# Turning the new convolution state on VectorE instead of TensorE, with its stores spread over steps

## The chip, the cores and the metric

The kernel runs on one core of a Trainium2 chip. The core has a matrix engine (TensorE, "PE" in the profile, with its weight loads shown apart as "PEld"), VectorE ("DVE"), ScalarE ("ACT"), GpSimd ("POOL") and SyncE ("SP"), which here only requests DMA transfers. Each engine works through its own queue of instructions in order; an instruction that needs a result of another engine or of a DMA waits at the head of its queue, and all that stands behind it waits too. The metric is the device time of one execution in microseconds (us).

## What is computed

One layer of a streaming encoder is applied to 256 new frames of one stream (the prompt) and to 16 new frames of each of 8 running streams (the sample), 384 rows of 2048 features in all. What matters here is the convolution branch:

```
u   = glu_in[..., :D_CONV] * jax.nn.sigmoid(glu_in[..., D_CONV:])
ext = jnp.concatenate([conv_buf, u], axis=1)            # 30 old rows, then the new ones
z   = layernorm(causal_dwconv(ext, conv_dw_w, conv_dw_b), ...)   # 31 taps, each channel by itself
new_conv = ext[:, -(CONV_W - 1):]                       # the last 30 rows are an output
```

D_CONV is 1024. For the prompt the last 30 rows of `ext` are its last 30 frames. For a sample stream they are 14 old rows and the 16 new ones. Around this stand an input projection, attention, two gates, an output projection and a feed-forward part; all matrix products are made in float32 accuracy, each as three products of a high and a low part.

## The kernel before, in words

The input projection is done panel by panel. Weights come as tiles of 256 rows by 512 columns: SP requests the load into one of three `raw` buffers (line 157), ACT rounds it to the high part `hi` (line 176), DVE subtracts to get the low part `lo` (line 177), and TensorE multiplies `hi` and `lo` (lines 313 to 315, or 318 to 320). There are three buffers for each of `hi` and `lo` (in the GLU stage below a fourth pair in every fourth turn). One call of `gemm` runs over its jobs; after each row block of 128 weights it calls `tick`, which takes one step of the side works. Such a step is called a step here.

Two stages concern us. In the **GLU stage** the 1024 channels of `u` are made with channels on the partitions: four jobs of 16 steps, 12 products of 384 columns in each step, two chunks of 128 channels out of each job. `glu_evac` (lines 783 to 793) takes them out of PSUM on DVE, applies the sigmoid on ACT, and multiplies on POOL into `ut[:, c, :]`, chunk c of eight: 128 channels by 384 rows, the 256 prompt frames first, then 8 streams of 16. Side works of this stage are the attention (`attention`, line 759, a head begins every sixth step) and the convolution (`conv`, line 799). In the **gate stage** after it the two gates are made in eight jobs of 16 steps, nine products of 512 columns in each step; the convolution goes on as a side work and the layer norm over it follows (`conv_branch`, line 932).

The convolution takes chunk c of eight in its turn, 17 steps after the chunk before. `load_state` (line 802) brings the old rows into `sc` by four DMAs 16 steps ahead. `fill` (line 810) builds `ext`, one of two buffers: it transposes `sc` in 32x32 blocks on DVE (line 812) and copies `ut` with shifts on ACT and POOL (lines 814 to 818). It then makes the new state, as channels must become columns: TensorE multiplies two pieces of `ut[:, c]` with the identity into a PSUM tile of the kind `misc` (lines 821 and 822), ACT copies both to `su` (lines 823 and 824), and SP requests two stores to the outputs (lines 825 and 826). Three steps later come the 31 taps, one a step: `tap` (line 828) multiplies a shifted view of `ext` by a column and adds it to `ut[:, c]` on DVE (line 833 for the first tap, 835 for the others). The first tap writes `ut[:, c]`, which is also what lines 821 and 822 read.

TensorE's order is the order of the program text (`tc.manual_schedule(engines={ENG.PE})`, line 381). On the other engines a scheduler orders the instructions when the kernel is built: it simulates the engines, and each engine takes, of what is ready then, the instruction that stands first in the program, where `tc.high_priority` lets the splits, the attention and the evacuations stand some hundred instructions further ahead. On the chip the order is fixed. So DVE's taps need not run in their step: they may come earlier than TensorE's step of the same number, if what they read is there.

The feed-forward part, from about 800 us on, has an order of its own made by a planner; the change does not touch it.

Of the kernel before, what the change touches and what calls it, by code (L numbers as in the profile page):

```python
# [8 lines left out]
F32 = mybir.dt.float32  # L9
# [6 lines left out]
P = 128  # L16
# [25 lines left out]
def hybrid_step(  # L42
# [9 lines left out]
    nc = tc.nc  # L52

    def pool(name, side="left", bufs=1, space=None):
        kw = dict(name=name, bufs=bufs, reuse_waits="tile")
        if space is not None:
            kw["space"] = space
        else:
            kw["side"] = side
        cm = tc.tile_pool(**kw)  # L60
        p = cm.__enter__()
        return p, lambda: cm.__exit__(None, None, None)
# [15 lines left out]
    def misc_tile():  # L78
        made[1] += 1
        return misc.tile([P, 512], F32, tag="misc", name="misc")  # L80
# [13 lines left out]
    tr = nc.tensor.transpose  # L94
# [11 lines left out]
    def queued(d, chain=True):  # L106
        e = d.ins.engine
        if chain and e in newest:
            tc.add_manual_dep(d.ins, newest[e], mybir.DependencyInfo(
                mybir.DependencyClass.NoSync, mybir.DependencyReason.DATA), reason="queue")  # L110
        newest[e] = d.ins.name
# [9 lines left out]
    ident = cp.tile([P, P], F32, name="ident")  # L121
# [306 lines left out]
    p_cv, close_cv = pool("conv", side="right")  # L428
# [116 lines left out]
    def tiny(name):  # L545
        return p_qkv.tile([P, NTT, H], F32, name=name)

    z, e, r, s2, pl = tiny("lz"), tiny("le"), tiny("lr"), tiny("ls"), tiny("lpoly")
# [230 lines left out]
    ut = p_cv.tile([P, 8, NT], F32, name="ut")  # L779
# [17 lines left out]
    nc.gpsimd.memset(sc[:], 0.0)  # L797

    def conv():
        exts = {}  # L800

        def load_state(c):
            for a in range(4):
                o = c * P + 32 * a
                d = nc.sync.dma_start(sc[32 * a:32 * a + 30], state_conv[0, :, :, o:o + 32]
                                      .rearrange("b r d -> r b d"))
                if c == 0:
                    queued(d)

        def fill(c):  # L810
            ext = exts[c] = p_cv.tile([P, 24, 46], F32, tag="ext", bufs=2, name="ext")
            nc.vector.transpose(ext[:, 16:24, 0:32], sc[:])
            u3 = ut[:, c, :].rearrange("p (a t) -> p a t", t=16)
            nc.scalar.copy(ext[:, :, 30:46], u3)
            nc.gpsimd.memset(ext[:, 0, 0:30], 0.0)
            nc.gpsimd.memset(ext[:, 1, 0:14], 0.0)
            nc.scalar.copy(ext[:, 1:16, 14:30], u3[:, 0:15, :])
            nc.scalar.copy(ext[:, 2:16, 0:14], u3[:, 0:14, 2:16])
            su = p_cv.tile([P, 2, P], F32, tag="su", bufs=1, name="su")
            ps = misc_tile()  # L820
            tr(ps[:, :P], ut[:, c, 2 * P:], ident[:])
            tr(ps[:32, P:2 * P], ut[:, c, 224:256], ident[:])
            nc.scalar.copy(su[:, 0, :], ps[:, :P])
            nc.scalar.copy(su[:32, 1, :], ps[:32, P:2 * P])
            nc.sync.dma_start(sample_conv[0, :, 14:30, c * P:(c + 1) * P], su[:, 0, :])
            nc.sync.dma_start(prompt_conv[0, 0, :, c * P:(c + 1) * P], su[2:32, 1, :])

        def tap(c, w):
            v = exts[c][:, :, w:w + 16]
            o = ut[:, c, :].rearrange("p (a t) -> p a t", t=16)  # L830
            wc = cw[:, w * 8 + c:w * 8 + c + 1]
            if w == 0:
                ts(o, v, wc, col[:, R_DWB + c:R_DWB + c + 1], op0=ALU.mult, op1=ALU.add)
            else:
                stt(o, v, wc, o, op0=ALU.mult, op1=ALU.add)  # L835
            if w == CW - 1:
                if c == 1:
                    nc.gpsimd.tensor_tensor(sm[:], ut[:, 0, :], ut[:, 1, :], op=ALU.add)
                elif c > 1:
                    nc.gpsimd.tensor_tensor(sm[:], sm[:], ut[:, c, :], op=ALU.add)  # L840

        for t in range(-CONV_FIRST, 7 * CONV_LAG + CW):
            for c in range(8):
                w = t - c * CONV_LAG
                if w == -16:
                    load_state(c)
                elif w == -3:
                    fill(c)
                elif 0 <= w < CW:
                    tap(c, w)  # L850
            yield

    conv_steps = conv()
    extra.append(p_att)
    load_k(0)
# [811 lines left out]
```

## Time and profile before

| | us |
|---|---|
| median of three runs | 1937.66 (1937.37 to 1938.39) |
| the profiled execution's own time | 1938.61 |
| its span, first to last instruction | 1936.9 |
| GLU stage in the span, about | 212 to 382 |
| gate stage in the span, about | 382 to 640 |

The profile is of one execution. Its busy times by engine, its stretches and its timelines are counted from the start of the span. A row of the timeline has the start, the duration, the engine, the line, the operation, what is written and read, the count of merged instructions, and in brackets the idle time before it with what ended it. A row of the groups has a line, engine and operation, the shapes, the count, then busy time and mean duration in ns. A row of one line's instructions has the shortest, median and longest duration in ns. A row of stretches has the stretch, its length, then each engine's busy time with its number of instructions, TensorE's granted clock as a share, the share of time in which the DMA engines were busy, and GB/s. The granted clock of TensorE was 1.000 over the span.

### The profile page before, as it was taken

The page shows a single profiled execution, that of the slowest core. Times are in us where ns is not written, and L with a number is a line of the kernel's source. Part 1 is how long each engine was busy: PE and PEld are TensorE (multiplying, and loading weights), DVE is VectorE, ACT ScalarE, POOL GpSimd, SP SyncE. Part 2 cuts the span into 40 slices and gives each one's busy share as a digit, 9 for nine tenths or more (in the row PEclk, how much of TensorE's full clock was granted, in tenths as well). Part 3 has the DMA queues.
Part 4 walks back from the last instruction along what each step waited for, and adds up shares of the span by engine and source line. Part 5 has one row for each costly group of instructions (what it writes and reads, how often), then busy time and mean ns, then how long its engine had stood idle before and what let it go on. Part 6 is the DMA issues. An engine that isn't in the chain of part 4 may idle for free.

```text
span 1936.9 us, 25423 instructions
## 1 busy us (share of the span) xinstructions
PE 1928.4 (100%) x9132; PEld 1629.3 (84%) x9132; DVE 1556.1 (80%) x2131; ACT 932.5 (48%) x1322; POOL 151.0 (8%) x298
## 2 busy tenths in 40 slices
PE   9999999999999999999999999999999999999999
PEld 9888999988888888888888888888888888888887
DVE  4446979888864568677699989898999999999985
ACT  5444454433333522344556464555555555555552
POOL 2000001100000000000101010101010101101010
PEclk9999999999999999999999999999999999999999
DMA  6564677454444343634545454545454545545453
GB/s 185 156 184 119 211 166 167 136 148 126 132 132 130 121 130 129 205 124 130 154 147 164 145 164 149 153 152 162 133 164 151 165 152 155 166 139 177 134 162 138
DMA packets 220721, 293.37 MB, mean 151 GB/s; under 512 B 59354, under 2 KB 105109, under 8 KB 220587
## 3 DMA queue, kind: packets, MB, share of 16 engines
q1 hardware_dynamic: 213395, 281.74, 49.1%
q0 software_dynamic: 7168, 10.00, 2.0%
q8 instruction: 71, 1.16, 0.3%
q14 instruction: 55, 0.45, 0.1%
q10 hardware_dynamic: 32, 0.01, 0.0%
HBM read 266.98 MB, written 7.86 MB: 142 GB/s over the span
## 4 chain that ended last, share of the span: by engine, by line
PE 96%; DVE 2%; DMA 1%; issue 0%; SPq 0%; ACT 0%; ACTq 0%; DVEq 0%
PE bank L1412 17%; PE bank L1411 17%; PE bank L1410 17%; PE acc L320 8%; PE acc L318 8%; PE acc L319 8%; PE misc L320 4%; PE misc L318 4%; PE misc L319 4%; PE acc L313 2%; PE acc L315 2%; PE acc L314 2%; DMA raw<-in_w_down_dram 0%; DVE mixT L337 0%; DVE lo L177 0%
## 5 line engine op out<-in xcount | busy, mean ns | idle before, releaser
L1103 ACT CAST hi<-raw 128x1024 fp32r<-128x1024 f32 x260 | 270.3, 1051 | 316.1 <-DVE raw L1103 140.3
L177 DVE TENSOR_TENSOR lo<-raw,hi 128x1024 fp32r<-128x1024 f32 (+2 forms) x219 | 259.5, 1187 | 194.7 <-ACT hi L176 192.5
L176 ACT CAST hi<-raw 128x1024 fp32r<-128x1024 f32 (+2 forms) x219 | 221.7, 1012 | 387.9 <-PE misc L320 300.6
L1103 DVE TENSOR_TENSOR lo<-raw,hi 128x1024 fp32r<-128x1024 f32 x260 | 314.7, 1221 | 48.2 <-ACT hi L1103 46.5
L318 PE MATMUL acc<-hi,hT 128*128 128x512 f32 (+1 forms) x512 | 193.1, 377 | 1.3 <-ACT hT L378 1.3
L320 PE MATMUL acc<-hi,hT 128*128 128x512 f32 (+1 forms) x512 | 190.5, 372 | 0.1
L319 PE MATMUL acc<-lo,hT 128*128 128x512 f32 (+1 forms) x512 | 190.1, 371 | 0.0
L1410 PE MATMUL bank<-hi,xg 128*128 128x512 f32 x440 | 171.2, 389 | 0.0
L1411 PE MATMUL bank<-lo,xg 128*128 128x512 f32 x440 | 171.2, 389 | 0.0
L1412 PE MATMUL bank<-hi,xg 128*128 128x512 f32 x440 | 171.2, 389 | 0.0
L835 DVE SCALAR_TENSOR_TENSOR ut<-ext,cw,ut 128x384 f32<-128x384 f32 x240 | 151.2, 630 | 6.0
L1412 PE MATMUL bank<-hi,act 128*128 128x512 f32 x396 | 154.2, 389 | 0.2 <-DVE act L1103 0.2
L1410 PE MATMUL bank<-hi,act 128*128 128x512 f32 x396 | 154.1, 389 | 0.0
L1411 PE MATMUL bank<-lo,act 128*128 128x512 f32 x396 | 154.0, 389 | 0.0
L1103 ACT CAST x21h<-raw 128x1024 fp32r<-128x1024 f32 x82 | 86.2, 1051 | 101.7 <-DVE raw L1103 50.1
L318 PEld LDWEIGHTS acc<-hi,hT 128*128 128x128 f32 x512 | 96.3, 188 | 16.6 <-ACT hT L378 1.6
L320 PEld LDWEIGHTS acc<-hi,hT 128*128 128x128 f32 x512 | 96.1, 188 | 15.5 <-DVE hT L379 0.5
L319 PEld LDWEIGHTS acc<-lo,hT 128*128 128x128 f32 x512 | 96.4, 188 | 14.9
L1103 DVE TENSOR_TENSOR x21l<-raw,x21h 128x1024 fp32r<-128x1024 f32 x82 | 100.2, 1222 | 7.8 <-ACT x21h L1103 6.7
L1411 PEld LDWEIGHTS bank<-lo,xg 128*128 128x128 f32 x440 | 82.6, 188 | 17.1
L1410 PEld LDWEIGHTS bank<-hi,xg 128*128 128x128 f32 x440 | 82.6, 188 | 17.1
L1412 PEld LDWEIGHTS bank<-hi,xg 128*128 128x128 f32 x440 | 82.6, 188 | 17.1
(393 smaller groups left out, 4277.1 us busy)
## 6 DMA issues: line engine op xcount, KB each, us to landing
raw<-in_w_up_dram SPq DMA_DIRECT2D x176, 512.0 KB
raw<-in_w_in_dram SPq DMA_DIRECT2D x96, 512.0 KB
raw<-in_w_down_dram SPq DMA_DIRECT2D x88, 512.0 KB
raw<-in_w_in_dram SPq DMA_DIRECT2D x64, 256.0 KB
raw<-in_w_out_dram SPq DMA_DIRECT2D x32, 512.0 KB
raw<-in_w_att_out_dram SPq DMA_DIRECT2D x16, 512.0 KB
raw<-in_conv_pw_out_dram SPq DMA_DIRECT2D x16, 512.0 KB
raw<-in_w_in_dram SPq DMA_DIRECT2D x23, 344.0 KB
```

Of the source, the lines that this page charges most:

```text
L176: queued(nc.scalar.copy(hi[:, k, :o], raw[:, k, :o]), first)
L177: queued(tt(lo[:, k, :o], raw[:, k, :o], f(hi[:, k, :o]), op=ALU.subtract), first)
L313: mm(o, hi[:, kk, s], ah, start=st, stop=False)
L314: mm(o, hi[:, kk, s], al, start=False, stop=False)
L318: mm(o, ah[:, s], hi[:, kk, :n], start=st, stop=False)
L319: mm(o, ah[:, s], lo[:, kk, :n], start=False, stop=False)
L320: mm(o, al[:, s], hi[:, kk, :n], start=False, stop=sp)
L835: stt(o, v, wc, o, op0=ALU.mult, op1=ALU.add)
L1103: d = op(*args, **kw)
L1410: mm(o, ah, h[:, kk, :], start=start, stop=False, **kw)
L1411: mm(o, ah, l[:, kk, :], start=False, stop=False, **kw)
L1412: mm(o, al, h[:, kk, :], start=False, stop=stop, **kw)
```

## The change

The two products with the identity, their `misc` tile and the two ACT copies go. In their place DVE transposes `ut[:, c, 224:384]`, 128 channels by 160 rows, in 32x32 blocks straight into `su`, which becomes 128 x 5 x 32 elements with two buffers. A block transpose leaves the four groups of 32 channels on their own partitions: partition 32a+i, block q, column j holds row 224+32q+i of channel 32a+j. So the stores are cut too: for each group of 32 channels two stores of the sample (streams 0, 2, 4, 6 and streams 1, 3, 5, 7; 16 rows by 4 streams by 32 channels) and one of the prompt (30 rows by 32 channels), twelve for a chunk in place of two. They are requested in the steps of the taps 0 to 11, one a step, and each moves runs of 32 elements (128 bytes) where the old ones moved runs of 128 elements (512 bytes).

```diff
@@ def conv():
-        exts = {}
+        exts, sus = {}, {}
...
             nc.scalar.copy(ext[:, 1:16, 14:30], u3[:, 0:15, :])
             nc.scalar.copy(ext[:, 2:16, 0:14], u3[:, 0:14, 2:16])
-            su = p_cv.tile([P, 2, P], F32, tag="su", bufs=1, name="su")
-            ps = misc_tile()
-            tr(ps[:, :P], ut[:, c, 2 * P:], ident[:])
-            tr(ps[:32, P:2 * P], ut[:, c, 224:256], ident[:])
-            nc.scalar.copy(su[:, 0, :], ps[:, :P])
-            nc.scalar.copy(su[:32, 1, :], ps[:32, P:2 * P])
-            nc.sync.dma_start(sample_conv[0, :, 14:30, c * P:(c + 1) * P], su[:, 0, :])
-            nc.sync.dma_start(prompt_conv[0, 0, :, c * P:(c + 1) * P], su[2:32, 1, :])
+            su = sus[c] = p_cv.tile([P, 5, 32], F32, tag="su", bufs=2, name="su")
+            nc.vector.transpose(su[:].rearrange("p q j -> p (q j)"), ut[:, c, 224:384])
+
+        def store(c, k):
+            a, b = k // 3, k % 3
+            o = c * P + 32 * a
+            if b < 2:
+                nc.sync.dma_start(sample_conv[0, b:8:2, 14:30, o:o + 32].rearrange("q r j -> r q j"),
+                                  sus[c][32 * a + 16 * b:32 * a + 16 * b + 16, 1:5, :])
+            else:
+                nc.sync.dma_start(prompt_conv[0, 0, :, o:o + 32], sus[c][32 * a + 2:32 * a + 32, 0, :])
...
                     fill(c)
                 elif 0 <= w < CW:
                     tap(c, w)
+                if 0 <= w < 12:
+                    store(c, w)
             yield
```

## The prediction

> **What bounds the kernel now.** I read the page first: busy times, then the shares of the chain of work that ended last. Then the stretches, for the stages in which the changed lines run.
>
> ```profile
> span 1936.9 us, 25423 instructions
> ...
> PE 1928.4 (100%) x9132; PEld 1629.3 (84%) x9132; DVE 1556.1 (80%) x2131; ACT 932.5 (48%) x1322; POOL 151.0 (8%) x298
> ...
> PE 96%; DVE 2%; DMA 1%; issue 0%; SPq 0%; ACT 0%; ACTq 0%; DVEq 0%
> ```
>
> ```profile
> 212.00:382.00 170.00, 169.84 (x1213) 163.45 (x1213) 143.55 (x306) 80.77 (x149) 17.28 (x23) 1.00 0.68 171
> 382.00:640.00 258.00, 257.85 (x1147) 213.09 (x1147) 189.39 (x265) 94.73 (x128) 10.15 (x17) 1.00 0.46 132
> ```
>
> TensorE is the bound, in the whole and in both stages: it is idle for 0.16 us of the GLU stage and 0.15 us of the gate stage. What leaves TensorE's queue there shortens the kernel; what any other engine gains or loses counts only if TensorE comes to wait for it. The chain runs over DVE further on (758 to 781 us), but that piece starts from a TensorE result and moves with it:
>
> ```profile
> 758.46 0.24 PE acc L320
> ...
> 781.38 0.33 PE misc L966
> ```
>
> **What TensorE loses.** Sixteen products with the identity, two a chunk. Their duration overlaps with their neighbours', so I price them by starts. First a weight tile in the gate stage, 18 products from one L320 to the like one after it, without the pair; then one with it; then the pair in the GLU stage, behind other products with the identity.
>
> ```profile
> 394.07 0.39 PE L320 MATMUL acc<-hi,hT 128*128 128x512 f32 x1
> ...
> 398.15 0.39 PE L320 MATMUL acc<-hi,hT 128*128 128x512 f32 x1
> ```
>
> ```profile
> 502.31 0.39 PE L320 MATMUL acc<-hi,hT 128*128 128x512 f32 x1
> ...
> 503.90 0.27 PE L821 MATMUL misc<-ident,ut 128*128 128x128 f32 x1
> ...
> 506.67 0.39 PE L320 MATMUL acc<-hi,hT 128*128 128x512 f32 x1
> ```
>
> ```profile
> 314.13 0.27 PE L821 MATMUL misc<-ident,ut 128*128 128x128 f32 x1
> 314.24 0.27 PE L822 MATMUL misc<-ident,ut 128*32 128x128 f32 x1
> ```
>
> A tile takes 398.15 - 394.07 = 4.08 us, and 506.67 - 502.31 = 4.36 us with the pair: 0.28 us, rounded up by the two decimals; I take 0.27. In the GLU stage starts are 0.11 us apart: 0.22 us a pair. Chunks 0 to 2 have their pair in the GLU stage, 3 to 7 in the gate stage: 3 x 0.22 + 5 x 0.27 = **2.0 us less**. The bounds are 1.8 (0.22 for all eight) and 4.35 (16 durations of 0.272, as if none overlapped). The Trainium skill, TensorE: Matmul & The Clock Gate, Part 4: PE-mode transpose, puts a 128x128 transpose "in one kernel's context" at about 275 ns. The duration in the rows agrees, but their starts stand 0.11 us apart, so I keep the starts; at the page's figure the sum would be, as an estimate, 4.4 us.
>
> **What ACT loses, what DVE and SP gain.**
>
> ```profile
> L823 ACT COPY su<-misc x8: 255/264/271, 268.6 to 539.3; 128x128 f32<-128x128 f32 x8
> L824 ACT COPY su<-misc x8: 249/250/253, 268.7 to 539.4; 32x128 f32<-32x128 f32 x8
> L825 SPq DMA_DIRECT2D out_dram<-su x8: 614/633/2524, 270.1 to 539.8; - x8
> L826 SPq DMA_DIRECT2D out_dram<-su x8: 412/420/477, 270.8 to 540.5; - x8
> ```
>
> ```profile
> L812 DVE STREAM_TRANSPOSE ext<-sc x8: 404/446/447, 237.4 to 495.6; 128x256 f32<-128x256 f32 x8
> ```
>
> ```profile
> L692 DVE STREAM_TRANSPOSE kTs<-kc 128x1024 f32<-128x1024 f32 x7 | 8.7, 1240 | 0.0
> ```
>
> ACT loses 8 x (0.264 + 0.250) = 4.1 us; it is half idle, so that is worth nothing. DVE gains eight block transposes of 160 columns. From 256 columns (0.446) to 1024 (1.240) a column costs 1.03 ns, so one costs 0.446 - 96 x 0.00103 = 0.35 us, 2.8 us in all, under TensorE's products; it reads a `ut` that is finished by then, as ACT's shifted copies of it are. SP gains 96 requests for 16: 96 x 0.42 to 0.63 us = 40 to 60 us against 8.4, so 5.0 to 7.6 us in each chunk's 35 to 47 us. These are small transfers, 8 KB or 3.75 KB in runs of 128 bytes; the nearest row with such runs is the load of `sc`:
>
> ```profile
> L805 SPq DMA_DIRECT2D sc<-in_state_conv_dram x32: 323/425/1246, 225.3 to 463.9; - x32
> ```
>
> ```profile
> q1 hardware_dynamic: 213395, 281.74, 49.1%
> ```
>
> At 0.425 us it confirms the price of a request; its longest, 1.246 us, is the upper end. The DMA engines get 8 x 632 = 5056 packets in place of 1264. The mean packet of this queue is 1.3 KB and takes 0.491 x 1936.9 x 16 / 213395 = 0.071 us, so the new ones cost at most 5056 x 0.071 / 16 = 22 us of all sixteen, over some 280 us: 8 points on a share of 0.46 to 0.68. The lower end is nothing. The Trainium skill, DMA: Bandwidth & Descriptors, Specifications, speaks against the cut: below 512 bytes an engine reads, modifies and writes. No store in this trace shows it; twice my upper end would be, as an estimate, 45 us, and the share would still be under one.
>
> What these requests could delay is a weight fetch behind them. A `raw` buffer is asked for as soon as DVE's `lo` frees it, and is needed by the third `hi` after, 3 x 4.08 = 12.2 us after the last one started.
>
> ```profile
> SPq L157 <- DVE lo L177: 584.3, 183, 7.5
> ```
>
> ```profile
> 1878.66 4.20 DMA raw<-in_w_down_dram
> ```
>
> Of these 12.2 us, `hi` and `lo` take 2.3 (1.05 and 1.22, rows below), the request 0.4 and a transfer of this size 4.2: 5.3 us are left. One store in the way costs 0.4 to 0.6 of that, so nothing.
>
> **What goes besides: a gate.** This is the part that no busy time shows. The first tap of a chunk writes what the pair reads, so it waited for TensorE, whose order is fixed. The stretches below are of the taps (L835) alone, then one row of DVE's timeline.
>
> ```profile
> 270.00:306.00 36.00, 19.81 (x30) 1.00 0.65 147
> 306.00:314.00 8.00, 0.00 (x0) 1.00 0.96 230
> 314.00:350.00 36.00, 18.86 (x30) 1.00 0.68 159
> 350.00:361.00 11.00, 0.00 (x0) 1.00 0.45 126
> ...
> 434.00:462.00 28.00, 18.52 (x30) 1.00 0.44 133
> 462.00:469.00 7.00, 0.00 (x0) 1.00 0.62 167
> ```
>
> ```profile
> 434.49 0.48 DVE L833 TENSOR_SCALAR ut<-ext,cw,col 128x384 f32<-128x384 f32 x1 [2.02 <-PE misc L822]
> ```
>
> Thirty taps run in one burst, then none until the next pair is through. With the pair gone, DVE can go from one chunk to the next, held only by `ext`, `sc` and itself. The convolution ends earlier, which saves nothing, as its reader on TensorE stands in a fixed place. But pauses in which DVE caught up go too. In the burst, ACT's `hi` comes when TensorE frees a buffer, and DVE's `lo` should follow at once:
>
> ```profile
> 434.24 1.05 ACT L176 CAST hi<-raw 128x1024 fp32r<-128x1024 f32 x1 [3.03 <-PE misc L320]
> ...
> 458.95 1.05 ACT L176 CAST hi<-raw 128x1024 fp32r<-128x1024 f32 x1 [3.02 <-PE misc L320]
> ```
>
> ```profile
> 435.54 1.22 DVE L177 TENSOR_TENSOR lo<-raw,hi 128x1024 fp32r<-128x1024 f32 x1
> ...
> 444.10 1.22 DVE L177 TENSOR_TENSOR lo<-raw,hi 128x1024 fp32r<-128x1024 f32 x1
> 445.23 3.88 DVE L835 SCALAR_TENSOR_TENSOR ut<-ext,cw,ut 128x384 f32<-128x384 f32 x6
> 449.03 1.22 DVE L177 TENSOR_TENSOR lo<-raw,hi 128x1024 fp32r<-128x1024 f32 x1
> ...
> 461.05 1.85 DVE L177 TENSOR_TENSOR lo<-raw,hi 128x1024 fp32r<-128x1024 f32 x1
> ```
>
> The first `lo` starts 0.25 us after its `hi` (435.54 against 434.24 + 1.05), the one six tiles later 1.05 us after (461.05 against 458.95 + 1.05). So DVE falls back 0.80 / 6 = 0.13 us a tile, with 29 of the burst's 30 taps in six tiles, 4.83 each. With three pairs of buffers, that `lo` is due two tiles after TensorE's release, at 434.24 + 8.16 = 442.4, and was there at 435.54 + 1.22 = 436.8: 5.6 us to spare. Today the pause after each burst wipes the lag out. Without pauses:
>
> ```profile
> L835 DVE SCALAR_TENSOR_TENSOR ut<-ext,cw,ut 128x384 f32<-128x384 f32 x161 | 100.9, 626 | 4.5
> ```
>
> 161 taps run from 382 us on. If half of the GLU stage's two pauses (19 us) is filled, some 15 go there and 145 remain: 30 tiles, 30 x 0.13 = 3.9 us of lag (33 tiles and 4.3 us if none go there). That is under 5.6, so I cost the lost gate at **nothing**, with little to spare. In the GLU stage the attention pulls DVE back to TensorE's time within a burst, too:
>
> ```profile
> 339.80 0.29 DVE L746 COPY on<-misc 128x128 f32<-128x128 f32 x1 [0.20 <-PE misc L744]
> ```
>
> DVE waits for TensorE there, 26 us into a burst, so no lag is carried on; nothing again, though TensorE's one wait of 0.16 us, at the burst's end, says that a crowded head uses all its room.
>
> **Sum.** -2.0 us on TensorE, the rest covered. The profiled execution would go from 1938.6 to 1936.6; on the median of the runs, 0.95 us lower, 1937.7 - 2.0 = **1935.7**, which is 0.10% and within the 0.2% (3.9 us) that a measurement of this kernel can about tell from no change.
>
> **Rivals.**
> - *Paid back.* DVE's lag crosses its 5.6 us at an average of 4.93 taps a tile (29.4 tiles x (0.13 + 0.10 x 0.65) = 5.7, 0.65 us being a tap, 3.88 / 6), and eats the 2.0 us at 5.03. For it: the margin is thin. Against: today's order gives 4.83, and the lag goes wherever `ext` or `sc` still holds a chunk up. Time 1935.9 to 1940, about 1937.7.
> - *Slower: DVE's backlog.* Place: the gate stage, `lo` behind taps. A tile with six taps takes 449.03 - 444.10 = 4.93 us, 0.85 too long. At 5.35 taps on average the lag grows 0.13 + 0.52 x 0.65 = 0.47 us a tile, 27 tiles, 12.7 us; less the spare 5.6 and the 2.0 gained, +5.1: 1942.8. It decides from 5.03 taps on. For it: such a tile stands in the burst. Against: tiles of four make up for it.
> - *Slower: twelve stores in a row* ahead of a fetch. At 0.63 us they hold SP 7.6 us, 2.3 over its 5.3, which the 5.6 behind `hi` cover; at 1.246 us, 15.0 - 5.3 - 5.6 = 4.1 us a chunk, 33 - 2 = +31: 1969. Against: one a step, and SP's queue mostly waits for DVE (584 us).
> - *Faster: the pair cost its whole duration*, 16 x 0.272 = 4.35 us: 1933.3. The Trainium skill's page TensorE: Matmul & The Clock Gate, as cited above, would have it about so. The 4.36 us tile speaks against it. It would mean that TensorE hides a stall there that its starts don't show.
>
> **Numbers.** Forecast 0.58, paid back 0.22, backlog 0.13, stores 0.03, faster 0.04. So faster by over 0.2% 0.04, within 0.2% 0.80, slower 0.16. The range from 1934.9 (a gain of 2.8, a third of the way from 2.0 to 4.35) to 1941.0 leaves out the faster case, the stores and most of the backlog, 0.16. The forecast by itself holds 1935.0 to 1936.5.
>
> **What would show it.** TensorE's tiles at 4.08 us throughout the gate stage; idle TensorE still near 0.3 us over both stages; taps without the pauses of 7 to 11 us, the last one earlier; `lo` up to 4 us behind `hi`; 96 requests of about 0.42 to 0.63 us. Wrong if TensorE's rows get idle time ended by `lo` or by a fetch, or if the pauses remain, which would mean that something other than the pair held the taps.

## The result, and the profile after

| | before | after |
|---|---|---|
| median, 21 runs each | 1937.89 us (1937.12 to 1938.75) | 1940.47 us (1938.39 to 1943.30) |
| ratio, 95% interval | 1 | 1.0013 (1.0007 to 1.0019) |
| profiled execution | 1938.61 us | 1940.19 us |
| its span, granted clock | 1936.9 us, 1.000 | 1938.5 us, 0.999 |

The change makes the kernel slower by 2.6 us, 0.13%. That is within the 0.2% that the forecast called "no change", but on the other side of it: 2.0 us less was forecast, and the 1940.47 us lie inside the range only because it reached to the rivals.

The page of the changed kernel has the same shape: span and busy times.

```profile
span 1938.5 us, 25456 instructions
...
PE 1928.5 (99%) x9116; PEld 1628.1 (84%) x9116; DVE 1548.8 (80%) x2139; ACT 930.0 (48%) x1306; POOL 153.6 (8%) x298
```

TensorE has 16 instructions less and is busy as long as before, though the work that went was worth 2.0 us. The two stages, then the waits of TensorE's matmuls from 212 to 640 us (us in total, times, longest):

```profile
212.00:382.00 170.00, 167.53 (x1189) 160.82 (x1188) 144.45 (x315) 77.47 (x141) 15.97 (x23) 0.99 0.67 166
382.00:640.00 258.00, 258.00 (x1142) 213.28 (x1141) 179.56 (x262) 94.14 (x118) 13.64 (x17) 1.00 0.47 134
```

```profile
PE misc L740 <- DVE mx L717: 2.5, 1, 2.5
```

The idle time of both stages was to stay near 0.3 us. It is 2.5 us, all in the GLU stage, and it is one wait. That stage also shows a granted clock of 0.99. TensorE's timeline round the wait (start, duration, and in brackets the idle time before with what ended it):

```profile
353.91 0.34 PE L315 MATMUL acc<-hT,lo 128*128 128x384 f32 x1
356.72 0.59 PE L740 MATMUL misc<-vt,pT 128*128 128x128 f32 x2 [2.47 <-DVE mx L717]
357.25 1.08 PE L744 MATMUL misc<-vc,pz 128*32 128x128 f32 x16
```

L740 begins `head_out` of the seventh head. It writes a `misc` tile, which is free only when L717 on DVE has read the scores of the eighth and last head out of it. DVE's and ACT's timelines, and POOL's for the bias that L717 adds:

```profile
350.51 1.93 DVE L838 SCALAR_TENSOR_TENSOR ut<-ext,cw,ut 128x384 f32<-128x384 f32 x3
355.23 1.23 DVE L177 TENSOR_TENSOR lo<-raw,hi 128x1024 fp32r<-128x1024 f32 x1 [2.79 <-ACT hi L176]
356.38 0.28 DVE L717 CUSTOM_DVE_ANT_0 pr<-misc,bs 128x128 f32<-128x128 f32 x1
```

```profile
354.15 1.04 ACT L176 CAST hi<-raw 128x1024 fp32r<-128x1024 f32 x1 [4.19 <-PE acc L314]
```

```profile
353.00 0.46 POOL L685 TENSOR_TENSOR bs<-bs,mk 128x128 f32<-128x128 f32 x1
```

DVE stood idle for 2.79 us at the head of its queue, in front of a weight tile's `lo`. The bias was done at 353.46, so L717 could have run 2.9 us earlier, but it stood behind that `lo`. The `lo` waited for its `hi`, and the `hi` for TensorE to free a buffer, which it did at 354.1, with the last product but one before its own wait. In the kernel before, L717 ran before that `lo`:

```profile
351.34 0.29 DVE L717 CUSTOM_DVE_ANT_0 pr<-misc,bs 128x128 f32<-128x128 f32 x1 [0.43 <-POOL bs L684]
```

What has moved is the order of DVE's queue, fixed when the kernel is built. The last bias load is later as well. On SP, before (first fence) and after (second), it stands behind a weight fetch:

```profile
341.30 0.90 SPq L157 DMA_DIRECT2D raw<-in_w_in_dram  x2
342.63 0.34 SPq L678 DMA_DIRECT2D bs<-c_dr  x1
```

```profile
345.19 0.91 SPq L157 DMA_DIRECT2D raw<-in_w_in_dram  x2
346.20 0.41 SPq L678 DMA_DIRECT2D bs<-c_dr  x1
```

The requests themselves cost what was priced, and so does the transpose (shortest, median, longest in ns):

```profile
L826 SPq DMA_DIRECT2D out_dram<-su x64: 316/424/706, 280.2 to 467.0; - x64
L829 SPq DMA_DIRECT2D out_dram<-su x32: 380/435/2140, 288.1 to 467.5; - x32
L820 DVE STREAM_TRANSPOSE su<-ut x8: 326/336/346, 250.7 to 454.0; 128x160 f32<-128x160 f32 x8
```

To see where time goes I matched TensorE's products of two traces one by one, in the order of the program, the sixteen left out. The table has by how much a product starts later than in the kernel before (negative: earlier), at times of the kernel before. The first 20 us scatter by almost a microsecond from execution to execution and the last 40 us by more, so the column at 20 is the zero of its row, and I stop at 600.

| kernel | 20 | 318 | 353 | 360.5 | 390 | 475 | 525 | 600 | net |
|---|---|---|---|---|---|---|---|---|---|
| after | -0.81 | -1.17 | -1.39 | 2.88 | 2.69 | 1.89 | 2.03 | 1.77 | +2.58 |
| three stores | 0.22 | -0.13 | -0.36 | -0.36 | -0.56 | -1.36 | -0.57 | -0.82 | -1.04 |
| stores by POOL | 0.16 | -0.18 | 3.82 | 3.83 | 4.76 | 3.96 | 4.06 | 3.80 | +3.64 |
| short stores | -0.68 | -1.08 | -1.31 | 1.43 | 1.25 | 0.45 | 0.55 | 0.29 | +0.97 |
| order given | -0.48 | -0.82 | -1.05 | -0.73 | -0.75 | -1.55 | -0.29 | -0.54 | -0.06 |
| order, spread taps | 0.29 | -0.08 | -0.30 | -0.30 | 0.32 | -0.48 | -0.75 | -1.00 | -1.29 |
| order, all spread | 0.03 | -0.31 | -0.53 | -0.44 | -0.62 | -1.42 | -1.69 | -1.95 | -1.98 |

In the changed kernel the pairs come off as forecast (-0.36 by 318, -0.80 from 390 to 475). Between 353 and 360.5 it loses 4.27 us, and 0.14 between 475 and 525, where a pair of 0.26 should have been gained: 0.4 more. The other rows are six of the experiments.

### The profile page after: what moved, and what is told of

It reads as the page before. It is cut to its first block, busy times and chain, and to the rows that moved or that the text cites. A ratio compares the mean times of both kernels' runs of the same rounds, so it can differ in the third digit from the quotient of the medians.

```text
span 1938.5 us, 25456 instructions
## 1 busy us (share of the span) xinstructions
PE 1928.5 (99%) x9116; PEld 1628.1 (84%) x9116; DVE 1548.8 (80%) x2139; ACT 930.0 (48%) x1306; POOL 153.6 (8%) x298
## 4 chain that ended last, share of the span: by engine, by line
PE 95%; DVE 2%; DMA 1%; issue 1%; ACT 0%; SPq 0%; DVEq 0%; ACTq 0%
PE bank L1417 17%; PE bank L1415 17%; PE bank L1416 17%; PE acc L318 8%; PE acc L319 8%; PE acc L320 8%; PE misc L319 4%; PE misc L318 4%; PE misc L320 4%; PE acc L313 2%; PE acc L314 2%; PE acc L315 2%; DMA raw<-in_w_down_dram 0%; DVE mixT L337 0%; DVE lo L177 0%
## 5 line engine op out<-in xcount | busy, mean ns | idle before, releaser
L838 DVE SCALAR_TENSOR_TENSOR ut<-ext,cw,ut 128x384 f32<-128x384 f32 x240 | 143.4, 638 | 1.4
```

## The experiments

**Theory A**: the twelve requests on SP push the last bias load back, and the stall follows. **Theory B**: the lost gate does it, as DVE's taps, free of the pair, come at other places in its order.

**1. The gate kept.** The changed kernel with the pair on TensorE again; its product isn't used.

```diff
             su = sus[c] = p_cv.tile([P, 5, 32], F32, tag="su", bufs=2, name="su")
             nc.vector.transpose(su[:].rearrange("p q j -> p (q j)"), ut[:, c, 224:384])
+            ps = misc_tile()
+            tr(ps[:, :P], ut[:, c, 2 * P:], ident[:])
+            tr(ps[:32, P:2 * P], ut[:, c, 224:256], ident[:])
```

> The changed kernel, with the two products with the identity put back into the fill beside VectorE's transpose; their result is not used. The taps are gated by TensorE again, the twelve stores stay. Theory A (the stores): the requests on SyncE bring the last head's bias later, VectorE's order has a weight tile's low part ahead of that head's first score row, and TensorE waits about 2.5 us near 355 us and runs at a lower clock after it. Then the stall stays and the products cost their 2.0 us again: 1941.5 to 1943.5. Theory B (the lost gate: taps that run early change the order on VectorE): the stall goes, and the time is that of the kernel before, 1937.5 to 1938.3.

Measured: 1943.65 us, ratio 1.0029 (1.0018 to 1.0040), 0.15 us above A's upper end. The stall at L740 is there with its 2.5 us, and another stands at 334 us:

```profile
PE misc L740 <- DVE mx L717: 2.5, 1, 2.5
PE misc L711 <- DVE kTs L692: 1.8, 1, 1.8
```

**2. Three stores.** The changed kernel with the requests of taps 0 to 2 alone; the other nine stores of each chunk, three quarters of the new state, are left out.

```diff
-                if 0 <= w < 12:
+                if 0 <= w < 3:
```

> The changed kernel with the stores of taps 0 to 2 alone; nine of the twelve stores of each chunk are left out, so three quarters of the new state are not written. The gate is gone as in the changed kernel. Theory A (the stores): no stall near 355 us, idle TensorE of both stages under 0.5 us, 1935.5 to 1936.7. Theory B (the lost gate): the stall stays, about 2.5 us and the slower clock behind it, 1939.5 to 1941.5.

Measured: 1937.54 us, ratio 0.9996 (0.9986 to 1.0005), about 0.8 us above what A expected. TensorE's matmuls have no wait at all from 212 to 382 us, so the stall is gone, with the gate still lost. What is left over is in the gate stage: the table's row loses 0.79 us from 475 to 525, where a pair should have given 0.26.

**3. The stores alone.** The kernel before, pair and gate kept, with each chunk's stores cut into twelve and requested one a step.

```diff
-            nc.sync.dma_start(sample_conv[0, :, 14:30, c * P:(c + 1) * P], su[:, 0, :])
-            nc.sync.dma_start(prompt_conv[0, 0, :, c * P:(c + 1) * P], su[2:32, 1, :])
+        def store(c, k):
+            a, b = k // 3, k % 3
...
+                if 0 <= w < 12:
+                    store(c, w)
```

> The kernel before, products with the identity and ACT copies kept, with its two stores cut into twelve of the same sizes, one a step of the taps 0 to 11. Theory A (the stores): the stall near 355 us appears, 2 to 5 us over the kernel before: 1940 to 1943. Theory B (the lost gate): no stall, within 0.5 us of the kernel before, 1937.4 to 1938.4.

Measured: 1944.13 us, ratio 1.0027 (1.0016 to 1.0038), 1.1 us above A's upper end. Both stalls again:

```profile
PE misc L740 <- DVE mx L717: 2.5, 1, 2.5
PE misc L711 <- DVE kTs L692: 1.4, 1, 1.4
```

So the stores bring the stall without any other part of the change, and the lost gate doesn't bring it without them. B falls.

**4. The bias earlier.** The changed kernel with a head's bias load put right after the scores of the head two before, with the attention's priority.

```diff
-                if step is head_probs and d["h"] + 2 < H:
-                    load_b(d["h"] + 2)
+                if step is head_scores and d["h"] + 2 < H:
+                    with tc.high_priority(offset=ATT_AHEAD):
+                        load_b(d["h"] + 2)
```

> The changed kernel with one more edit: a head's bias is requested behind the scores of the head two before it, and with the attention's priority, not behind that head's probabilities at the usual one. Theory A (the stores push the last bias behind weight fetches): the stall near 355 us goes and the whole gain of 2.0 us shows, 1935.5 to 1936.5. Theory B (the lost gate, low parts late by themselves): no better than the changed kernel by over 1 us, 1939.5 to 1941.5.

Measured: 1944.71 us, ratio 1.0032 (1.0020 to 1.0045): slower still, which neither theory expected. L740 doesn't wait any more, but the products of two heads do (L711), both times for the transposed keys. The second row names L721, but what L711 reads is the keys' transposition, which ends at 355.01, and L711 starts at 355.06:

```profile
PE misc L711 <- DVE kTs L692: 2.8, 2, 2.7
PE misc L711 <- DVE mx L721: 1.8, 1, 1.8
```

Where the keys were waited for longest, the last of their four transfers had landed at 333.2 us, but their transposition stood in DVE's queue behind the first two reductions of the same head:

```profile
333.51 0.29 DVE L717 CUSTOM_DVE_ANT_0 pr<-misc,bs 128x128 f32<-128x128 f32 x1 [1.03 <-PE misc L703]
...
335.37 1.25 DVE L692 STREAM_TRANSPOSE kTs<-kc 128x1024 f32<-128x1024 f32 x1
```

So a load moved on SP turned the order of DVE's queue elsewhere. That split A into three: **O**, the order (requests shift the planned times, and an instruction that frees what TensorE waits for gets behind a `lo`); **Q**, SP's time on the chip (the bias lands late, whatever the order); **R**, the traffic of many small pieces. The next four runs tell them apart.

**5. Stores by POOL**, `nc.gpsimd.dma_start` in both stores; **6. Stores by ACT**, `nc.scalar.dma_start` in both.

> The changed kernel with its twelve stores per chunk requested by GpSimd instead of SyncE. In the order in which VectorE gets its instructions the last head's score reduction (L717) then stands ahead of the `lo` again, as before the change. Theory O (order: the requests on SyncE move the last head's bias load back in the planned order, so that a weight tile's `lo` is put ahead of that reduction, and TensorE's L740 waits for both): no stall near 354 us, the pairs' 2.0 us gained, 0.4 to 0.9 us given back to the backlog of VectorE in the gate stage: 1936.0 to 1937.5 us. Theory Q (the requests hold SyncE at run time, so the bias lands late, whatever the order): the same, since SyncE is free of them. Theory R (the transfers' many small pieces load the DMA engines): the stall of 2.5 us stays, 1939.5 to 1942 us.

> The changed kernel with its twelve stores per chunk requested by ScalarE. SyncE has none of them, but in VectorE's order the `lo` still stands ahead of the last head's reduction (L717). Theory O: the wait of TensorE's L740 stays, 1.5 to 3 us of it with a lower clock behind it, 1939.5 to 1942.5 us. Theory Q: SyncE is free, the bias lands early, no stall: 1936.0 to 1937.5 us. Theory R: stays, as with O. Should ScalarE's own 96 requests of 0.4 to 0.6 us show, they add waits of TensorE that end with ScalarE, which no theory here counts.

Measured: 1940.12 us for POOL (ratio 1.0010, 1.0001 to 1.0019), 1943.36 us for ACT (1.0027, 1.0018 to 1.0037). The first is a miss of O's number and of Q's; the second is 0.9 us above O's upper end and far from Q's. O's number for POOL had been worked out from the order round the last head alone. With POOL's requests the stall is two heads earlier, where the fifth head's L740 waits for the sixth head's reductions, and it is the same:

```profile
321.90 0.34 PE L315 MATMUL acc<-hT,lo 128*128 128x384 f32 x1
324.67 0.80 PE L740 MATMUL misc<-vt,pT 128*128 128x128 f32 x2 [2.43 <-DVE mx L717]
```

```profile
323.18 1.23 DVE L177 TENSOR_TENSOR lo<-raw,hi 128x1024 fp32r<-128x1024 f32 x1 [1.26 <-DMA bs<-c_dr]
324.32 0.28 DVE L717 CUSTOM_DVE_ANT_0 pr<-misc,bs 128x128 f32<-128x128 f32 x1
```

Again a `lo` directly ahead of L717. (The row names a bias load, but `lo` reads no bias; its `hi` ended at 323.14, and POOL had finished the sixth head's bias at 315.05.) With ACT's requests TensorE waits 3.18 us for the last head, though SP has none of the stores. But this run says nothing for O: ACT's own `hi` stands among its requests, SP asks for that bias as late as 351.16, and L717 starts 0.61 us after the `lo`, when POOL's L684 is done at 357.18. Here the late bias alone is enough for the stall.

```profile
355.36 1.23 DVE L177 TENSOR_TENSOR lo<-raw,hi 128x1024 fp32r<-128x1024 f32 x1 [0.45 <-ACT hi L176]
357.20 0.29 DVE L717 CUSTOM_DVE_ANT_0 pr<-misc,bs 128x128 f32<-128x128 f32 x1 [0.61 <-POOL bs L684]
```

Q in its simple form, that SP's time under the stores is what counts, falls with both.

**7. Short stores.** The changed kernel's twelve requests, each sample store with one stream of its four; the other three quarters of the sample's new rows are left out.

```diff
-                nc.sync.dma_start(sample_conv[0, b:8:2, 14:30, o:o + 32].rearrange("q r j -> r q j"),
-                                  sus[c][32 * a + 16 * b:32 * a + 16 * b + 16, 1:5, :])
+                nc.sync.dma_start(sample_conv[0, b:b + 1, 14:30, o:o + 32].rearrange("q r j -> r q j"),
+                                  sus[c][32 * a + 16 * b:32 * a + 16 * b + 16, 1:2, :])
```

> The changed kernel with the same twelve requests per chunk, but each sample store carries one stream of four, so three quarters of the first convolution's new sample state are left out: 16 pieces of 128 bytes instead of 64. The order of every engine is that of the changed kernel. Theories O and Q: nothing changes, stall of about 2.5 us at 354 us, 1939.5 to 1941.5 us. Theory R: without three quarters of the small pieces the stall goes, 1936.0 to 1938.0 us.

Measured: 1939.98 us, ratio 1.0009 (1.0000 to 1.0018). The stall is unchanged, so R falls:

```profile
356.81 0.49 PE L740 MATMUL misc<-vt,pT 128*128 128x128 f32 x2 [2.47 <-DVE mx L717]
357.23 0.65 PE L744 MATMUL misc<-vc,pz 128*32 128x128 f32 x16
```

**8. The order given.** The changed kernel with a dependency, without a wait on the chip, that keeps that one `lo` behind the last head's three reductions. Besides it only a tap, a copy and two reciprocals right behind change their places on DVE, and one instruction on ACT; the orders of SP and POOL are the same. The first two added lines stand in `head_scores`, where `t_` is the reduction L717, the others in `split_rows`, where `d` is the `lo`.

```diff
+            if d["h"] == H - 1 and i == 2:
+                last_score[:] = [2, t_.ins.name]
...
+        if last_score:
+            last_score[0] -= 1
+            if last_score[0] == 0:
+                tc.add_manual_dep(d.ins, last_score[1], mybir.DependencyInfo(
+                    mybir.DependencyClass.NoSync, mybir.DependencyReason.DATA), reason="order")
```

> The changed kernel with one order given: that `lo` comes after the three score reductions of the last head (L717) on VectorE. Nothing else in any engine's order changes, the requests stay on SyncE where they were, and the last bias load stays where it was too. Theory O: VectorE was idle for 2.8 us ahead of that `lo`, so the reductions run there, the wait of L740 goes with the low clock behind it: 1936.0 to 1937.5 us. Theories Q and R: the bias still lands late, the reduction can't start, at least 1 us of the stall stays: 1938.3 to 1940.5 us.

Measured: 1938.41 us, ratio 1.0000 (0.9992 to 1.0009): 2.1 us below the changed kernel, but 0.9 above what O expected. By its number it lies in the range of Q and R, too; but these expected at least 1 us of the stall to stay, and the rows decide. The stall itself is gone, as O said, while the bias is as late as before and L717 waits for it:

```profile
353.87 0.29 DVE L723 CUSTOM_DVE_ANT_0 pr<-misc,bs 128x128 f32<-128x128 f32 x1 [1.08 <-POOL bs L690]
...
355.58 1.23 DVE L177 TENSOR_TENSOR lo<-raw,hi 128x1024 fp32r<-128x1024 f32 x1 [0.59 <-ACT hi L176]
```

```profile
354.43 0.38 PE L748 MATMUL misc<-vt,pT 128*128 128x128 f32 x2
355.07 0.64 PE L752 MATMUL misc<-vc,pz 128*32 128x128 f32 x16 [0.25 <-DMA vc<-in_cache_v_dram]
```

(Lines stand six or eight further down: L723 is L717, L748 is L740, L752 is L744.) L748 doesn't wait. All that is left of the late loads is 0.25 us for the values (`vc`), which are requested behind the bias. So the place of one `lo` made the stall. What eats the gain now is in the gate stage, -1.55 at 475 and -0.29 at 525 in the table. Waits of TensorE's weight loads there, then DVE, ACT and TensorE at the worst place:

```profile
PEld acc L325 <- DVE lo L177: 2.3, 6, 0.9
```

```profile
482.16 3.79 DVE L846 SCALAR_TENSOR_TENSOR ut<-ext,cw,ut 128x384 f32<-128x384 f32 x7
485.87 1.22 DVE L177 TENSOR_TENSOR lo<-raw,hi 128x1024 fp32r<-128x1024 f32 x1
```

```profile
478.67 1.05 ACT L176 CAST hi<-raw 128x1024 fp32r<-128x1024 f32 x1
```

```profile
487.14 0.50 PE L325 MATMUL acc<-lo,hT 128*128 128x512 f32 x1 [0.45 <-DVE lo L177]
```

Counted back from 517 us, where `lo` follows its `hi` at once again, this `lo` belongs to the `hi` of 478.67: it comes 485.87 - 479.72 = 6.15 us behind it. This is the prediction's rival, DVE's backlog, in its small form.

**9 to 11. The taps spread.** To the given order comes a second one: from the fourth chunk on, each tap is kept behind a certain `lo`, so that fourteen taps stand to three weight tiles (9) or nine to two (11). In 10 the taps are spread as in 9, and the order at the last head is left as the change made it. The lines stand in `tap`, where `d` is the tap and `los` lists the `lo` so far.

```diff
+            if c >= 3:
+                pace[:] = [pace[0], pace[1] + 1] if pace else [len(los) - 2, 0]
+                tc.add_manual_dep(d.ins, los[min(pace[0] + pace[1] * 3 // 14, len(los) - 2)], mybir.DependencyInfo(
+                    mybir.DependencyClass.NoSync, mybir.DependencyReason.DATA), reason="pace")
```

> The changed kernel with the given order of the last run (the `lo` after the last head's three reductions) and, besides, VectorE's taps from the fourth chunk on spread over the weight tiles, fourteen to every three tiles, so that a `lo` never stands behind six or seven taps. Theory O with the backlog as the second cost: with the stall gone, what was left of the loss was 0.9 to 1.3 us of `lo` that came late at 480 to 515 us; 14 taps of 0.53 us and three `lo` of 1.14 us are 10.8 us of the 12.2 us that three tiles take, so it goes: 1936.0 to 1937.3 us, faster than the kernel before. Rival (the gain of the removed products is lost to something that no stall shows, a clock or a transfer): the time stays at that of the last run, 1937.8 to 1939.0 us.

> The changed kernel with the taps spread as in the run beside it, and the order round the last head left as the change has it. Theory O with the backlog as a second cost: the stall of 2.6 us at 354 us stays, with or without the lower clock behind it, and the 0.4 us of late `lo` goes: 1938.0 to 1940.3 us. Rival (spreading the taps alone cures it, the backlog being the whole loss): 1936.0 to 1937.3 us, as the run beside it.

> As the first run of this call with nine taps to every two tiles, so the convolution ends later still. If fourteen to three already leaves no `lo` late, nothing changes: within 0.5 us of that run, 1936.0 to 1937.5 us. If some backlog is left there, this one is faster by up to 0.5 us. Rival (the convolution's end is near what the stage behind it needs): slower than that run by over 1 us.

Measured: 1937.11 us (ratio 0.9995, 0.9987 to 1.0004), 1940.58 us (1.0016, 1.0007 to 1.0025) and 1937.35 us (0.9996, 0.9988 to 1.0005). Spreading alone leaves the stall (10; its median is 0.3 us above O's upper end). With the order it takes 1.3 us off run 8, and slower spreading adds nothing. No `lo` is waited for in the gate stage any more (-0.48 at 475, -0.75 at 525: the pair's gain stays). What still goes, 0.8 us at 381 us, is the same crowding at the end of the GLU stage, where the accumulator that TensorE needs is freed behind two taps (L796 is L787 of the changed kernel):

```profile
379.76 1.27 DVE L847 SCALAR_TENSOR_TENSOR ut<-ext,cw,ut 128x384 f32<-128x384 f32 x2
380.94 1.01 DVE L796 TENSOR_TENSOR sgb<-acc,rs1b 128x384 f32<-128x384 f32 x2
```

```profile
381.55 0.50 PE L325 MATMUL acc<-hi,hT 128*128 128x512 f32 x1 [0.52 <-DVE sgb L796]
```

**12. All spread.** As 9, with the third chunk's taps four to a tile.

```diff
+            if c == 2:
+                pace2[:] = [pace2[0], pace2[1] + 1] if pace2 else [len(los) - 4, 0]
+                tc.add_manual_dep(d.ins, los[min(pace2[0] + pace2[1] * 1 // 4, len(los) - 2)], mybir.DependencyInfo(
+                    mybir.DependencyClass.NoSync, mybir.DependencyReason.DATA), reason="pace")
```

> The kernel with the given order and fourteen taps to three tiles, and the third chunk's taps spread too, four to a tile, so that the two products of VectorE that free TensorE's accumulators at the end of the GLU stage (L787 in the changed kernel) do not stand behind its backlog: there TensorE still waited 0.7 to 0.8 us at 381 us. Theory O with the backlog as the second cost: that wait goes, all of the pairs' 2.0 us is kept: 1936.0 to 1936.9 us, below the kernel before in every interval. Rival (the last two tenths of a per cent are the scatter of the start and the end of the run): no difference from the version without this, 1936.8 to 1937.6 us.

Measured: **1936.38 us** against 1938.37 for the kernel before in the same runs, ratio 0.9989 (0.9980 to 0.9998). It is below the kernel before by the 2.0 us that the prediction had worked out, and below the changed one as well: the table's last row gains 1.98 us, and TensorE is idle for 0.03 and 0.15 us of the two stages.

```profile
212.00:382.00 170.00, 169.97 (x1211) 163.49 (x1210) 143.82 (x313) 80.37 (x145) 17.32 (x24) 1.00 0.70 171
382.00:640.00 258.00, 257.85 (x1143) 213.45 (x1142) 184.43 (x270) 94.28 (x119) 9.77 (x17) 1.00 0.47 134
```

It is 0.1%, less than I would call sure from a single comparison; the rows and the time agree.

## Why the prediction was wrong

*The pairs, -2.0 us: right, with a little luck.* In every trace without the pair each shows as 0.17 to 0.19 us in the GLU stage and, where no late `lo` falls on it, 0.25 or 0.26 in the gate stage. That makes 1.8 us for eight, a little under what was forecast; the wait of 0.16 us near 350 us, which I hadn't counted as a gain, went with them and fills the sum up to 2.0.

*Requests of 0.42 to 0.63 us, transposes of 0.35, small transfers that don't show: sized right.* The median request took 0.42 to 0.44 us, the transpose 0.34, and the run with a quarter of each sample store gained nothing that can be measured.

*"One store in the way costs 0.4 to 0.6 of that, so nothing": this step failed.* I asked whether SP has time for 96 requests and what stands behind one, with the queues as the trace of before had them. I didn't ask what else changes its place when 96 instructions enter the plan from which the order of every other queue comes. Their price was nothing; the order that they left cost 2.5 us of idle TensorE, and 4.3 in the trace with the low clock behind it. Two things on record could have pointed there. The text before the prediction says that the order is made by a simulation when the kernel is built. And of TensorE's wait of 0.16 us I wrote that it "says that a crowded head uses all its room", having just cost the GLU stage at "nothing again". None of the rivals had this mechanism: "twelve stores in a row" looked for the loss in a late fetch, and no fetch was late for TensorE.

*The lost gate: the mechanism was right, the cost too small.* The taps do run without pauses and end earlier. The stretches of L838 alone, after:

```profile
440.00:470.00 30.00, 21.70 (x40) 1.00 0.48 132
...
515.00:570.00 55.00, 0.00 (x0) 1.00 0.49 144
```

40 taps in 30 us are 5.4 to a tile, not the 4.83 that I took from today's order. At my 0.65 us a tap that would have been the rival at 1942.8 and worse. It wasn't, because the taps became cheaper. Before (first fence) one chunk's taps follow each other; after (second) two chunks take turns in DVE's queue (the fifth chunk's first tap stands at 410.67, and POOL's sum over the fourth, which waits for its last tap, at 423.69), until the last chunk is alone again:

```profile
453.79 3.23 DVE L835 SCALAR_TENSOR_TENSOR ut<-ext,cw,ut 128x384 f32<-128x384 f32 x5
```

```profile
416.50 3.79 DVE L838 SCALAR_TENSOR_TENSOR ut<-ext,cw,ut 128x384 f32<-128x384 f32 x7
...
421.35 2.73 DVE L838 SCALAR_TENSOR_TENSOR ut<-ext,cw,ut 128x384 f32<-128x384 f32 x5
...
505.72 3.23 DVE L838 SCALAR_TENSOR_TENSOR ut<-ext,cw,ut 128x384 f32<-128x384 f32 x5
```

Five taps and six (the prediction's row of 3.88 us) are 0.65 us apart, five and seven in turns 1.06 us: 0.53 us a tap. So the two errors, the count and the duration, work against each other. A third does not: I let the lag grow from nothing at 382 us. In the kernel before, in the burst ahead of the one that I read, a `lo` already started 2.46 us behind its `hi` (425.46 against 421.95 + 1.05), and in run 8 it is 1.7 us at 387. The lag came to 6.15 us in run 8 where 3.9 was forecast, just over the 5.6 us to spare, which was right. Its price, the loss from 475 to 525 with the pair in that stretch added, is 0.4 us after the stall (changed kernel, short stores), and 1.1 to 1.5 us where there was none (three stores, order given). That the stall gave DVE time to catch up would explain the difference; it was only argued.

*What stays open:* why the scheduler turned just these places. Twelve requests a chunk on any of three engines turned one, three a chunk on SP didn't, and one load moved turned another. That it is the bias's or the keys' planned time that decides is likely from where they stand, but the scheduler's own times are in no trace.

## What to carry to other kernels

Where a build-time scheduler fixes the queues, an instruction that costs nothing can still cost time by what it reorders: after each change look first for new waits of the bounding engine, then ask which instruction stands ahead of the one that ended the wait, and whether it had to. If the order is to blame, give that one order explicitly and keep the change; moving the load that looked late only moved the stall (run 4), and moving the requests to another engine did so too (run 5). A forecast for such a kernel should hold a rival "the order turns somewhere", priced by the tightest spots of the trace, the places where the bounding engine already waits a little.

## What the runs showed of the hardware

The same wait of 2.47 us was sometimes followed by a lower clock. Stretches from 354 to 362 us of the changed kernel (first) and of the one with short stores (second), whose order is the same; the share after the instruction counts is the granted clock:

```profile
354.00:362.00 8.00, 5.53 (x38) 4.64 (x37) 5.67 (x20) 3.85 (x10) 0.00 (x0) 0.79 0.82 217
```

```profile
354.00:362.00 8.00, 5.53 (x46) 4.89 (x46) 6.54 (x22) 3.80 (x10) 0.20 (x1) 1.00 0.77 209
```

At 0.79 the sixteen products of L744 take 1.08 us, at 1.00 they take 0.65, and from 353 to 360.5 us the one execution loses 4.27 us and the other 2.74: the low clock is another 1.5 us. The 21 runs of the changed kernel fall apart in the same way: five with a mean granted clock of 1.000 took 1938.39 to 1939.06 us, the sixteen with 0.998 or 0.999 took 1939.88 to 1943.30. This is why one wait of 2.5 us can cost 2.5 or 4.

The other thing is the tap: taps of one chunk, each of which reads what the one before it wrote, started 0.65 us apart; where taps of two chunks took turns, each started 0.53 us after the one of the other chunk.
